# Attention scores: the low-query product on half the array, two query blocks at a time

## The chip, the cores and the metric

The kernel runs on one core of one Trainium2 chip. The metric is device time in microseconds of one execution. A core has TensorE (PE, the matrix multiplier, with its weight loads listed apart as PEld), VectorE (DVE), ScalarE (ACT), GpSimd (POOL) and SyncE (SP, whose queue issues the DMAs). Matmuls read SBUF and write banks of PSUM.

## The reference

One decoder layer for 2048 tokens of width 1024: a norm, one input projection, a causal convolution group beside an attention group, an output projection and a gated feed-forward part. Only the attention's scores are touched. Attention has 8 heads of 64 channels and no softmax:

```python
z = jnp.einsum("bhqd,bhkd->bhqk", qb, kh) * scale
mask = key_pos[None, :] < q_pos[:, None]
log_beta = jax.nn.log_sigmoid(z)
log_1m_beta = jnp.where(mask, jax.nn.log_sigmoid(-z), 0.0)
between = lax.cumsum(log_1m_beta, axis=3, reverse=True) - log_1m_beta
attn = jnp.where(mask, jnp.exp(log_beta + between), 0.0)
return jnp.einsum("bhqk,bhkd->bhqd", attn.astype(vh.dtype), vh)
```

So each query's weights over its keys follow from a running product of 1 - sigmoid(z), from the nearest key backwards.

## The kernel before

Precision: matmuls run on float32 in a rounded form (F32R). A value is split into a high part, rounded, and a low part, what is left; most products are the sum of three matmuls, high-high, high-low and low-high.

Tiling: tokens go in four groups of 512 (`G`, `NG`), each of four blocks of 128 (`TT`). The main stream of PE's work is written by `PLAN`: input projections of a group (`inproj`, lines 624 to 628), output projections (lines 1060 to 1062), first products of the feed-forward part (`c11`, `p4`, line 1124). Beside it run side streams at a set pace: attention (`attn`), the convolution's taps on VectorE (line 845), and sums of weights on GpSimd.

Attention of group g goes by units: one head h and one key group c, from c = g down to 0. There are 80 units, each of four query blocks. `begin(h)` loads the queries Q of a head (line 909), `fetch(h, c)` loads keys K and values V (lines 916 and 917). `scores(u, j)` makes one query block's 128 x 512 scores z in a bank of PSUM (two buffers) with two matmuls, lines 927 and 928, takes a sigmoid of it on ScalarE (line 930) and scans it on VectorE (line 933 on the diagonal, line 935 off it) into a row `om`, of which there are `NOM` buffers. On the diagonal (c = g), block j has (j + 1) x 128 columns. The scan starts with the last column of the same block's scan in the unit before. `values(u, b)` transposes a unit's four rows, 128 columns of each at a time (line 953), splits the result (lines 616 and 617) and multiplies it with V into o (lines 958 and 959). Values lag one unit behind scores.

In DRAM the keys of two heads lie in `kd[p, g]`, 128 channels by (high, low) by 512 tokens; `inproj` writes them with one DMA for the high half and one for the low (line 826). K is read so that its 128 partitions hold channel 0 high, channel 0 low, channel 1 high and so on. Q has each query channel on two neighbouring partitions, for the high half and, beside it, the low half of the queries. So one matmul over 128 partitions gives low queries times (high + low keys), the other high queries times (high + low keys).

The order in which instructions stand on every engine is worked out at build time, once, by a list scheduler (`Graph`, `forward`, `backward`, `arrange`). It works with a cost for each instruction (`cost`), with delays between engines, with a model of the DMAs, and with the buffers of each tile (`grant`): an instruction whose tile finds no free buffer is set aside. `in_order` then fixes that order. `o.after` are the instructions that must have ended before o, `o.behind` those of its own engine that must have been issued before it.

After scores and values end, some 1030 us of the span remain: the last output projection and the feed-forward part, which the diff doesn't touch.

Of the kernel before, what the change touches and what calls it, by code (L numbers as in the profile page):

```python
# [10 lines left out]
F32 = mybir.dt.float32  # L11
F32R = mybir.dt.float32r
# [7 lines left out]
P = 128  # L20
# [12 lines left out]
CW = 31  # L33
PAD = CW - 1
EPS = 1e-6
NOM = 8

PLAN = (
    ("prep", 0, 6, ("scaled", 0, 0, 0)),
# [100 lines left out]
HOP = 60.0  # L140
FLIGHT = 8
ROUNDS = 12
OVER = (("attn", "late"), ("mixed", "ffnt"), ("psum", "fpsum"))


# [51 lines left out]
def cost(i, kind, eng, ins, outs):  # L197

    n = width(outs[0])
    if kind == "InstMatmult":  # L200
        if size_of(ins[0].dtype) == 4 and not str(ins[0].dtype).endswith("r"):
            return 109, 270
        b = max(width(ins[0]) * 0.443, 109)
        return b, b + 165
    src = [place(a) for a in ins]
    if eng == "Activation":
        b = n * 0.833 + (49 if src[0] == "PSUM" else 94) + (93 if len(ins) > 1 else 0)
        return b, b + 115
    if eng == "DVE":
        if kind == "InstTensorScalarPtr":  # L210
            if i.is_tensor_tensor_scan:
                b = 2.04 * n + 140
            elif i.is_scalar_tensor_tensor:
                b = 1.04 * n + 125
            else:
                b = 1.04 * n + 160 if place(outs[0]) == "PSUM" else 0.73 * n + 113
        elif kind == "InstBNStatsAggregate":
            b = 93
        elif kind in ("InstTensorReduce", "InstBNStats"):
            b = 1.04 * width(ins[0]) + 48  # L220
        elif kind == "InstTensorTensor":
            b = 1.04 * n + 60
        else:
            b = n + 100
        return b, b + 100
    if kind == "InstTensorTensor" and n >= 16:
        b = 2.35 * n + 35
    elif "pow" in str(getattr(i, "op", "")):
        b = 375 + 150 * n
    else:  # L230
        b = 125 if n < 16 else 215
    return b, b + 65
# [7 lines left out]
class Op:  # L240
    def __init__(self, n, ins, eng, dma, busy, late, size, wide):
        self.n, self.ins, self.eng, self.dma, self.wide = n, ins, eng, dma, wide
        self.busy, self.late, self.size = busy, late, size
        self.after, self.behind, self.tiles = set(), set(), set()


class Graph:


    def __init__(self, insts):  # L250
        self.ops, self.root, self.order, self.users = [], {}, {}, {}
        seen = {}
        for i in insts:
            kind = type(i).__name__
            ins = [a for a in i.ins if hasattr(a, "bass_ap")]
            outs = [a for a in i.outs if hasattr(a, "bass_ap")]
            if not outs:
                continue
            eng, dma = str(i.engine).split(".")[-1], kind == "InstDMACopy"
            busy, late = (ISSUE, 0) if dma else cost(i, kind, eng, ins, outs)  # L260
            o = Op(len(self.ops), i, eng, dma, busy, late, width(outs[0]) * int(outs[0].ap[0][1]) * 4,
                   eng in ("DVE", "Pool") and not dma and in_sbuf(eng, ins, outs))
            uses = [(a.bass_ap.tensor, box(a), place(a), w) for aps, w in ((ins, False), (outs, True)) for a in aps
                    if hasattr(a.bass_ap.tensor, "tag_meta")]
            for t, b, sp, w in uses:
                if sp != "DRAM" and t.name not in o.tiles:
                    o.tiles.add(t.name)
                    self.users.setdefault(t.name, []).append(o.n)
                    if t.name not in self.root:
                        self.root[t.name] = t  # L270
                        self.order.setdefault(t.tag, []).append(t.name)
                writes, reads = seen.setdefault(t.name, ([], []))
                for old, lst in ((True, writes), (False, reads if w else ())):
                    for q, c, wrote in lst:
                        if sp == "PSUM" or meet(b, c):
                            same = q.eng == eng and not q.dma
                            (o.behind if same and (eng == "PE" or not (old and wrote)) else o.after).add(q.n)
            for t, b, sp, w in uses:
                writes, reads = seen[t.name]
                if sp == "PSUM":  # L280
                    writes[:] = [e for e in writes if e[0].eng != eng] + [(o, b, w)]
                elif w:
                    writes[:] = [e for e in writes if not holds(b, e[1])] + [(o, b, True)]
                    reads[:] = [e for e in reads if not holds(b, e[1])]
                else:
                    reads.append((o, b, False))
            o.behind -= o.after
            self.ops.append(o)
        for low, high in OVER:
            under = {o.n for o in self.ops if any(self.pool(x) == low for x in o.tiles)}  # L290
            for x in self.root:
                if self.pool(x) == high:
                    for n in self.roots(x):
                        self.ops[n].after |= {q for q in under if q < n} - self.ops[n].behind
        self.slots()
# [24 lines left out]

    def forward(self, ops, prio, slots=True):

        need = [len(o.after) + len(o.behind) for o in ops]
        fin = [{} for _ in ops]
        iss = [[] for _ in ops]
# [171 lines left out]
def layer_kernel(ctx: ExitStack, tc: tile.TileContext, x, xT, g_pre_mix, w_in, conv_w, conv_b, ln_g, ln_b,  # L497
# [183 lines left out]
    for g in range(NG):  # L681
        for p in range(CB):
            qd[p, g] = dp.tile([P, 2, G], F32R, name=f"qd{p}_{g}")
            kd[p, g] = dp.tile([P, 2, G], F32R, name=f"kd{p}_{g}")
            vd[p, g] = dp.tile([P, 2, G], F32R, name=f"vd{p}_{g}")

    done = set()
# [90 lines left out]
    def inproj(g, order):  # L778
# [6 lines left out]
        for n, (kind, c) in enumerate(order):  # L785
# [34 lines left out]
            else:  # L820
                H = ev("qkH", F32R)
                L = ev("qkL", F32R)
                split(ps, H, L)
                to = (qd if kind == "q" else kd)[c, g]
                for a, t in enumerate((H, L)):
                    nc.sync.dma_start(to[:, a, :].bitcast(F32), t.bitcast(F32))
            if kind != "v":
                done.add((kind, g, c))
            yield 1
# [70 lines left out]
    def attn(g):  # L900
# [4 lines left out]
        def begin(h):  # L905
            Q = ap.tile([P, 2, G], F32R, tag="Q", name="Q")
            half = qd[h // 2, g][h % 2 * DH:(h % 2 + 1) * DH]
            for i in range(2):
                nc.sync.dma_start(Q[slice(i, P, 2), :, :].bitcast(F32), half.bitcast(F32))
            return dict(Q=Q, prev=[lower[:, 0:1]] * TT, o=None)  # L910

        def fetch(h, c):
            K = ap.tile([P, G], F32R, tag="K", name="K")
            V = ap.tile([P, G], F32R, tag="V", name="V")
            half = kd[h // 2, c][h % 2 * DH:(h % 2 + 1) * DH].rearrange("p a t -> (p a) t")
            nc.sync.dma_start(K.bitcast(F32), half.bitcast(F32))
            nc.sync.dma_start(V.bitcast(F32), vd[h // 2, c][:, h % 2, :].bitcast(F32))
            return dict(h=h, c=c, K=K, V=V, A=[])

        def scores(u, j):  # L920
            hd_ = heads[u["h"]]
            diag = u["c"] == g
            w = (j + 1) * P if diag else G
            K = u["K"]
            z = pp.tile([P, G], F32, tag="z", name="z")
            js = slice(j * P, (j + 1) * P)
            nc.tensor.matmul(z[:, 0:w], hd_["Q"][:, 1, js], K[:, 0:w], start=True, stop=False)  # L927
            nc.tensor.matmul(z[:, 0:w], hd_["Q"][:, 0, js], K[:, 0:w], start=False, stop=True)  # L928
            om = ap.tile([P, G], F32, tag="om", name="om", bufs=NOM)
            nc.scalar.activation(z[:, 0:w], z[:, 0:w], AF.Sigmoid, scale=-0.125)  # L930
            r, zr = (t[:, 0:w][:, ::-1] for t in (om, z))
            if diag:
                nc.vector.tensor_tensor_scan(r, lower[:, G - w:G][:, ::-1], zr, hd_["prev"][j], ALU.add, ALU.mult)
            else:
                nc.vector.tensor_tensor_scan(r, zr, one.to_broadcast([P, w]), hd_["prev"][j], ALU.mult,  # L935
                                             ALU.bypass)
            hd_["prev"][j] = om[:, 0:1]
            if w == P and g:
                hd_["prev"][j] = sp.tile([P, 1], F32, tag="pv", name="pv", bufs=2)
                nc.gpsimd.tensor_tensor(hd_["prev"][j], om[:, 0:1], lower[:, G - P - 1:G - P], ALU.add)  # L940
            u["A"].append(om)
            return w
# [56 lines left out]
        for n in range(len(units) + 1):  # L999
# [6 lines left out]
                u = fetch(h, c)  # L1006
            for i in range(TT):
                w = 0
                if u is not None:
                    w += scores(u, i)  # L1010
                if last is not None:
                    w += values(last, i)
# [795 lines left out]
```

## Time and profile before

| what | value |
| --- | --- |
| time, median of 3 runs | 2353.0 us (2352.53 to 2353.67) |
| the profiled execution | 2352.9 us, span 2351.1 us |
| granted TensorE clock | 0.999 |
| score matmuls, lines 927 and 928 | 320 each, from 66 to 1315 us |
| K and V loads | 80 each, 256 KB |
| data moved by DMA | 656.66 MB |

The page lists an engine's busy time as a share of the span. Matmuls overlap in the array and their ends are modelled, so a matmul's own duration is longer than the time after which the next one can follow. The chain that ended last follows the work back from the last instruction, at each step to what released it; in order of time it shows how long each link of the chain took. A table by stretch gives each engine's busy time between two moments, the granted clock, the share of time in which the DMA engines were busy, and GB/s.

### The profile page before, as it was taken

The page shows a single profiled execution, that of the slowest core. Times are in us where ns is not written, and L with a number is a line of the kernel's source. Part 1 is how long each engine was busy: PE and PEld are TensorE (multiplying, and loading weights), DVE is VectorE, ACT ScalarE, POOL GpSimd, SP SyncE. Part 2 cuts the span into 40 slices and gives each one's busy share as a digit, 9 for nine tenths or more (in the row PEclk, how much of TensorE's full clock was granted, in tenths as well). Part 3 has the DMA queues.
Part 4 walks back from the last instruction along what each step waited for, and adds up shares of the span by engine and source line. Part 5 has one row for each costly group of instructions (what it writes and reads, how often), then busy time and mean ns, then how long its engine had stood idle before and what let it go on. Part 6 is the DMA issues. An engine that isn't in the chain of part 4 may idle for free.

```text
span 2351.1 us, 33675 instructions
## 1 busy us (share of the span) xinstructions
PE 2328.0 (99%) x11156; PEld 1926.8 (82%) x11156; DVE 1720.7 (73%) x2125; ACT 1176.6 (50%) x2102; POOL 1228.2 (52%) x1046
## 2 busy tenths in 40 slices
PE   8999999999999999999999999999999999999998
PEld 6888888888888878888888888888888888888886
DVE  7996899799997899856631268788666564557556
ACT  5457565575564555566564544334232335454543
POOL 4574357523552434335300257679876445478556
PEclk9999999999999999999999999999999999999999
DMA  9989886988698899977598868899998667668765
GB/s 372 310 312 314 300 286 209 348 303 289 226 342 299 285 348 333 331 238 237 180 348 259 271 230 304 301 317 334 366 338 279 207 241 228 195 197 299 228 190 179
DMA packets 277646, 656.66 MB, mean 279 GB/s; under 512 B 32864, under 2 KB 33376, under 8 KB 277472
## 3 DMA queue, kind: packets, MB, share of 16 engines
q1 hardware_dynamic: 277472, 654.51, 81.6%
q8 instruction: 88, 1.44, 0.2%
q14 instruction: 86, 0.70, 0.1%
HBM read 460.40 MB, written 193.99 MB: 278 GB/s over the span
## 4 chain that ended last, share of the span: by engine, by line
PE 96%; DVE 2%; POOL 1%; issue 1%; DMA 0%; ACT 0%; SPq 0%; POOLq 0%; DVEq 0%
PE b L1124 21%; PE dps L1124 17%; PE c L1124 10%; PE inps L624 6%; PE inps L628 6%; PE inps L626 6%; PE at L953 5%; PE z L928 3%; PE o L958 3%; PE o L959 3%; PE z L927 3%; PE p L1124 3%; PE ops L1060 3%; PE ops L1062 3%; PE ops L1061 2%; PE pf L974 1%
## 5 line engine op out<-in xcount | busy, mean ns | idle before, releaser
L845 DVE SCALAR_TENSOR_TENSOR cv<-glu,cw,cv 128x512 f32<-128x512 f32 x464 | 347.7, 749 | 9.5
L1414 POOL TENSOR_TENSOR wL<-raw,wH 128x512 fp32r<-128x512 f32 x176 | 266.3, 1537 | 148.8 <-ACT wH L1413 137.6
L1644 DVE TENSOR_TENSOR xL__19905<-t__19907,xH__19904 128x512 fp32r<-128x512 f32 x154 | 199.7, 1298 | 159.0 <-ACT xH__19904 L1643 158.7
L1642 POOL TENSOR_TENSOR xL__19903<-t__19906,xH__19902 128x512 fp32r<-128x512 f32 x154 | 208.5, 1356 | 157.5 <-ACT xH__19902 L1641 156.1
L617 DVE TENSOR_TENSOR TL<-at,TH 128x512 fp32r<-128x512 f32 (+1 forms) x320 | 189.3, 599 | 122.2 <-ACT TH L616 109.0
L578 ACT ACTIVATE wH<-raw 128x1024 fp32r<-128x1024 f32 x156 | 165.4, 1060 | 214.7 <-PE inps L628 105.5
L624 PE MATMUL inps<-xH,wL 128*128 128x512 f32 x640 | 257.8, 403 | 1.0 <-DVE glu L797 0.4
L626 PE MATMUL inps<-xH,wH 128*128 128x512 f32 x640 | 254.6, 398 | 0.0
L628 PE MATMUL inps<-xL,wH 128*128 128x512 f32 x640 | 254.3, 398 | 0.0
L935 DVE TENSOR_TENSOR_SCAN om<-z,om,one 128x512 f32<-128x512 f32 x168 | 212.8, 1274 | 42.9 <-ACT z L930 38.7
L1124 PE MATMUL dps<-xH__19902,xL__19905 128*128 128x512 f32 x616 | 239.8, 389 | 0.2 <-DVE xL__19905 L1644 0.2
L1124 PE MATMUL dps<-xH__19902,xH__19904 128*128 128x512 f32 x616 | 239.5, 389 | 0.0
L1124 PE MATMUL dps<-xL__19903,xH__19904 128*128 128x512 f32 x616 | 239.1, 389 | 0.0
L616 ACT ACTIVATE TH<-at 128x512 fp32r<-128x512 f32 (+1 forms) x320 | 167.9, 532 | 90.7 <-PE at L953 81.8
L930 ACT ACTIVATE z<-z 128x512 f32<-128x512 f32 (+2 forms) x320 | 167.4, 528 | 70.8 <-PE z L928 66.6
L1641 ACT ACTIVATE xH__19902<-t__19906 128x512 fp32r<-128x512 f32 x154 | 97.2, 631 | 205.5 <-POOL xL__19903 L1642 162.5
L582 POOL TENSOR_TENSOR wL<-raw,wH 128x1024 fp32r<-128x1024 f32 x46 | 110.5, 2402 | 149.0 <-ACT wH L578 122.2
L1413 ACT ACTIVATE wH<-raw 128x512 fp32r<-128x512 f32 x176 | 101.7, 624 | 163.7 <-PE b L1124 55.8
L953 PE MATMUL at<-idr,om 128*128 128x128 f32 x1088 | 180.8, 273 | 0.5 <-DVE om L935 0.4
L953 PEld LDWEIGHTS at<-idr,om 128*128 128x128 f32 x1088 | 136.4, 140 | 34.7 <-DVE om L935 0.9
L1208 POOL TENSOR_TENSOR sum<-sum 128x512 f32<-128x512 f32 x88 | 115.1, 1308 | 60.0 <-DMA sum<-in_w_gate_dram 40.7
L1124 PE MATMUL c<-xH,wL 128*128 128x512 f32 x352 | 140.8, 401 | 0.1
(296 smaller groups left out, 6014.0 us busy)
## 6 DMA issues: line engine op xcount, KB each, us to landing
wL<-wL SPq DMA_DIRECT2D x156, 512.0 KB, 5.2
raw<-in_w_in_dram SPq DMA_DIRECT2D x80, 512.0 KB, 6.1
t__19907<-u SPq DMA_DIRECT2D x154, 256.0 KB, 3.1
c<-c SPq DMA_DIRECT2D x88, 256.0 KB, 4.7
t__19906<-wd SPq DMA_DIRECT2D x88, 256.0 KB, 2.7
K<-kd SPq DMA_DIRECT2D x80, 256.0 KB, 4.6
V<-vd SPq DMA_DIRECT2D x80, 256.0 KB, 4.3
u<-accf SPq DMA_DIRECT2D x22, 768.0 KB, 6.7
```

Source lines behind the costliest of these rows:

```text
L616: nc.scalar.activation(H, ps, AF.Copy)
L617: nc.vector.tensor_tensor(L, ps, H.bitcast(F32), ALU.subtract)
L624: nc.tensor.matmul(ps, WL[:, kc], aH[t](k), start=k == 0, stop=False)
L626: nc.tensor.matmul(ps, WH[:, kc], aH[t](k), start=False, stop=False)
L628: nc.tensor.matmul(ps, WH[:, kc], aL[t](k), start=False, stop=k == KT - 1)
L845: nc.vector.scalar_tensor_tensor(to, gl[c][:, k:k + G], cw[:, c, k:k + 1], a, ALU.mult, ALU.add)
L935: nc.vector.tensor_tensor_scan(r, zr, one.to_broadcast([P, w]), hd_["prev"][j], ALU.mult, ALU.bypass)
L953: nc.tensor.transpose(pt[:, j * P:(j + 1) * P], u["A"][j][:, b * P:(b + 1) * P], id32)
L1124: return nc.tensor.matmul(ps, a, b, skip_group_check=True, **flags)
L1414: nc.gpsimd.tensor_tensor(l, t, f32(h), sub)
L1642: nc.gpsimd.tensor_tensor(WL, w, f32(WH), sub)
L1644: nc.vector.tensor_tensor(UL, t, f32(UH), sub)
```

## The change

The two matmuls of a block become a full and a half one. K's 128 partitions now hold the 64 high key channels and below them the 64 low ones; Q has the query channels twice, on partitions 0 to 63 and 64 to 127. High queries meet all 128 partitions, as before in sum. Low queries meet high keys alone, 64 partitions; the product of low queries and low keys is left out. `scores` is called for two blocks at a time: first the high matmul of either block, then the low matmul of block j on partitions 0 to 63, and that of block j + 1 on partitions 64 to 127, for which a second copy of the high keys (`KX`, two buffers) is loaded there. The two low matmuls write different banks. `NOM` goes from 8 to 6. Keys lie in DRAM by head (`kd[h, g]`), so that each tile of them is written by four DMAs. The scheduler takes a matmul whose operand starts above partition 0 as beside the matmul ahead of it, keeps it directly behind that one, and reckons 15 ns for it (`BESIDE`).

```diff
-NOM = 8
+NOM = 6
+BESIDE = 15.0
...
     if kind == "InstMatmult":
...
+        if box(ins[1])[0]:
+            return BESIDE, BESIDE + 165
...
+            if kind == "InstMatmult" and box(ins[1])[0]:
+                o.beside = True
+                last.after |= o.after
+                last.behind |= o.behind - {last.n} - last.after
+                last.behind -= last.after
+                o.after, o.behind = set(), {last.n}
+            if eng == "PE":
+                last = o
...
+        if slots:
+            prio = [float("-inf") if o.beside else prio[o.n] for o in ops]
...
-            kd[p, g] = dp.tile([P, 2, G], F32R, name=f"kd{p}_{g}")
+            for h in (2 * p, 2 * p + 1):
+                kd[h, g] = dp.tile([P, G], F32R, name=f"kd{h}_{g}")
...
-                to = (qd if kind == "q" else kd)[c, g]
                 for a, t in enumerate((H, L)):
-                    nc.sync.dma_start(to[:, a, :].bitcast(F32), t.bitcast(F32))
+                    if kind == "q":
+                        nc.sync.dma_start(qd[c, g][:, a, :].bitcast(F32), t.bitcast(F32))
+                        continue
+                    for h in range(2):
+                        nc.sync.dma_start(kd[2 * c + h, g][a * DH:(a + 1) * DH, :].bitcast(F32),
+                                          t[h * DH:(h + 1) * DH, :].bitcast(F32))
...
-                nc.sync.dma_start(Q[slice(i, P, 2), :, :].bitcast(F32), half.bitcast(F32))
+                nc.sync.dma_start(Q[slice(i * DH, (i + 1) * DH), :, :].bitcast(F32), half.bitcast(F32))
...
-            half = kd[h // 2, c][h % 2 * DH:(h % 2 + 1) * DH].rearrange("p a t -> (p a) t")
-            nc.sync.dma_start(K.bitcast(F32), half.bitcast(F32))
+            nc.sync.dma_start(K.bitcast(F32), kd[h, c].bitcast(F32))
+            KX = ap.tile([P, G], F32R, tag="KX", name="KX", bufs=2)
+            nc.sync.dma_start(KX[DH:P, :].bitcast(F32), kd[h, c][0:DH, :].bitcast(F32))
...
-            w = (j + 1) * P if diag else G
-            K = u["K"]
-            z = pp.tile([P, G], F32, tag="z", name="z")
-            js = slice(j * P, (j + 1) * P)
-            nc.tensor.matmul(z[:, 0:w], hd_["Q"][:, 1, js], K[:, 0:w], start=True, stop=False)
-            nc.tensor.matmul(z[:, 0:w], hd_["Q"][:, 0, js], K[:, 0:w], start=False, stop=True)
+            Q, K, KX = hd_["Q"], u["K"], u["KX"]
+            zs = []
+            for i in (j, j + 1):
+                w = (i + 1) * P if diag else G
+                z = pp.tile([P, G], F32, tag="z", name="z")
+                zs.append((i, w, z, slice(i * P, (i + 1) * P)))
+            for i, w, z, js in zs:
+                matmul(z[:, 0:w], Q[:, 0, js], K[:, 0:w], start=True, stop=False)
+            for (i, w, z, js), hp, k in zip(zs, (slice(0, DH), slice(DH, P)), (K, KX)):
+                matmul(z[:, 0:w], Q[hp, 1, js], k[hp, 0:w], start=False, stop=True)
+            return sum([scan(u, hd_, diag, *z) for z in zs])
+
+        def scan(u, hd_, diag, j, w, z, js):
             om = ap.tile([P, G], F32, tag="om", name="om", bufs=NOM)
...
-                if u is not None:
+                if u is not None and i % 2 == 0:
                     w += scores(u, i)
```

More of the change, by code (lines that the diff above doesn't have):

```diff
@@ L243, in __init__ @@
         self.busy, self.late, self.size = busy, late, size
-        self.after, self.behind, self.tiles = set(), set(), set()
+        self.after, self.behind, self.tiles, self.beside = set(), set(), set(), False
 class Graph:
@@ L914, in fetch @@
             V = ap.tile([P, G], F32R, tag="V", name="V")
-            half = kd[h // 2, c][h % 2 * DH:(h % 2 + 1) * DH].rearrange("p a t -> (p a) t")
-            nc.sync.dma_start(K.bitcast(F32), half.bitcast(F32))
+            nc.sync.dma_start(K.bitcast(F32), kd[h, c].bitcast(F32))
+            KX = ap.tile([P, G], F32R, tag="KX", name="KX", bufs=2)
+            nc.sync.dma_start(KX[DH:P, :].bitcast(F32), kd[h, c][0:DH, :].bitcast(F32))
             nc.sync.dma_start(V.bitcast(F32), vd[h // 2, c][:, h % 2, :].bitcast(F32))
-            return dict(h=h, c=c, K=K, V=V, A=[])
+            return dict(h=h, c=c, K=K, KX=KX, V=V, A=[])
         def scores(u, j):
```

## The prediction

> **What bounds the kernel now.** I read the page first: busy time by engine, then the chain that ended last.
>
> ```profile
> PE 2328.0 (99%) x11156; PEld 1926.8 (82%) x11156; DVE 1720.7 (73%) x2125; ACT 1176.6 (50%) x2102; POOL 1228.2 (52%) x1046
> PE 96%; DVE 2%; POOL 1%; issue 1%; DMA 0%; ACT 0%; SPq 0%; POOLq 0%; DVEq 0%
> PE z L927 <- DVE om L935: 0.8, 2, 0.5
> ```
>
> The matmuls make up 96% of the chain. The third row, from the list of who waited for whom, says that scores waited for a free bank of PSUM twice, 0.8 us in all. A busy PE is a modelled figure, so the next view is the table by stretch, which shows whether the other engines leave room where scores run (66 to 1315 us).
>
> ```profile
> core 0: us, PE busy (x) PEld busy (x) DVE busy (x) ACT busy (x) POOL busy (x), PEclk, DMA share, GB/s
> 66.00:1315.00 1249.00, 1245.94 (x6364) 1033.93 (x6363) 999.99 (x1356) 707.13 (x1274) 515.00 (x505) 1.00 0.85 289
> 200.00:1000.00 800.00, 798.03 (x4109) 661.27 (x4108) 730.44 (x991) 454.04 (x818) 355.64 (x346) 1.00 0.87 299
> 800.00:1000.00 200.00, 198.26 (x1000) 162.62 (x1000) 188.02 (x249) 102.06 (x181) 81.26 (x50) 1.00 0.95 330
> 1000.00:1315.00 315.00, 315.00 (x1561) 261.26 (x1560) 148.91 (x181) 178.73 (x312) 78.02 (x82) 1.00 0.75 252
> ```
>
> PE is idle for 3.1 of 1249 us. VectorE is 91% busy from 200 to 1000 (730.44 of 800), 94% in the last 200 of these, and has room only after 1000. So a microsecond taken from PE's stream in this stage is a microsecond of the end, as long as VectorE and the DMAs follow.
>
> How much stream time one matmul takes is read from the chain in order of time (start, length, what), not from an instruction's own duration, which holds the latency too:
>
> ```profile
> 702.37 0.12 PE z L927
> 702.49 0.12 PE z L928
> 703.24 0.18 PE z L928
> 1315.46 3.18 PE c L1124 x14
> 1318.64 0.44 PE at L953 x4
> 1319.08 2.09 PE c L1124 x9
> 1312.24 2.32 PE c L1124 x10
> 1325.94 3.00 PE c L1124 x13
> ```
>
> 512 columns take 3.18 / 14 = 0.227 us; z of 384 columns takes 0.18 (703.24), of 256 takes 0.12 (702.37), and a transpose of 128 columns 0.44 / 4 = 0.11. The granted clock is 1.00 in all these stretches, so no term changes with it.
>
> **The matmuls that go beside each other.** The groups by form count them:
>
> ```profile
> L927 PE MATMUL z<-K,Q 128*128 128x512 f32 x224 | 94.0, 419 | 0.9 <-DVE om L935 0.8
> L927 PE MATMUL z<-K,Q 128*128 128x384 f32 x32 | 11.9, 373 | 0.0
> L927 PE MATMUL z<-K,Q 128*128 128x256 f32 x32 | 10.3, 323 | 0.0
> L927 PE MATMUL z<-K,Q 128*128 128x128 f32 x32 | 7.7, 240 | 0.0
> ```
>
> There are 320 score blocks, each with a low and a high matmul (L928 has the same counts). The number of matmuls stays. The high ones keep 128 partitions and the stacked high and low keys; each low one drops to 64 partitions and loses the low-low product. Two neighbouring blocks make a pair, and the second low one sits on the other partition half, with no data in common with the first. If they run at once, a pair costs the longer of the two. Per head and key group off the diagonal there are two pairs of 512 and 512 columns: 224 less the 32 diagonal ones is 192 blocks, 96 pairs, saving 0.227 each: 21.8 us. On the diagonal, 32 pairs of 384 and 512 save the 384 one, 0.18 each: 5.8 us. 32 pairs of 128 and 256 save the 128 one, taken at a transpose's 0.11: 3.5 us. Together 31.1 us over 160 pairs: the most that there is.
>
> No instruction of before uses half the array (all forms read 128*128), so whether halves overlap, and at what price, is bounded. There are two unknowns.
>
> First, the second half's own weight load. Loads in the trace, near a stretch of transposes:
>
> ```profile
> 1318.25 0.58 PEld L953 LDWEIGHTS at<-idr,om 128*128 128x128 f32 x4
> 1318.81 0.19 PEld L1124 LDWEIGHTS c<-xH,wL 128*128 128x128 f32 x1
> 1318.92 0.19 PEld L1124 LDWEIGHTS c<-xH,wH 128*128 128x128 f32 x1
> 1319.15 0.19 PEld L1124 LDWEIGHTS c<-xL,wH 128*128 128x128 f32 x1
> ```
>
> Two loads can start 0.11 us apart (1318.81, 1318.92), though behind a long matmul each follows at the matmul's 0.23. So the second low matmul starts between 0 and 0.11 late. I take 0: the last high matmul streams for 0.227 in most pairs, and two loads of 0.11 fit under it. The other end is 160 x 0.11 = 17.6 us.
>
> Second, going from the whole array to halves and back. The nearest row is PE's other change of work, four transposes between plain matmuls: after them nine matmuls take 2.09 us where 9 x 0.227 = 2.04 is due, ten take 2.32 for 2.27, thirteen 3.00 for 2.95. A visit costs 0.05. The far end is that the pipe empties at each change: a matmul lasts 0.39 from start to end while its successor comes 0.23 later, so 0.16 a change and 0.32 a pair:
>
> ```profile
> 1304.30 0.39 PE L927 MATMUL z<-K,Q 128*128 128x512 f32 x1
> 1304.52 0.39 PE L928 MATMUL z<-K,Q 128*128 128x512 f32 x1
> ```
>
> The near end is nothing, as halves need not stop anything. I take 0.05, the one price of a change that the trace holds: 160 x 0.05 = 8.0 us.
>
> The rule that speaks against the change stands in the Trainium skill, TensorEngine Tiling (Array Packing), Key Properties: changing the tiling mode drains the engine. No run shown here changes it; at 0.16 a drain the sum would be 31.1 - 51.2, a loss of 20 us, which is the first rival. The page TensorE: Matmul & The Clock Gate, "Measured speedup vs the span model", has tiles on different rows starting about 4 ns apart: an estimate of 160 x 0.004 = 0.6 us for the second halves, against my 0.
>
> **The other parts.** *The order on PE.* The first high, the second high, then both low; the planner sets the second low matmul directly behind the first. Both banks of z are now held together: the next pair's first high matmul needs the first scan done, the low ones need both. Between the end of a pair's second scan and the next pair's first scan lie high, low and latency (0.23 + 0.39) and a sigmoid, some 1.2 us. What bears this is time per unit of four blocks: 80 units between 66 and 1315 us, 15.6 us each.
>
> ```profile
> L935 DVE TENSOR_TENSOR_SCAN om<-z,om,one 128x512 f32<-128x512 f32 x168 | 212.8, 1274 | 42.9 <-ACT z L930 38.7 <-PE at L953 3.3
> L617 DVE TENSOR_TENSOR TL<-at,TH 128x512 fp32r<-128x512 f32 x224 | 151.1, 680 | 103.6 <-ACT TH L616 91.9 <-PE o L959 8.5 <-PE at L953 1.4
> L930 ACT ACTIVATE z<-z 128x512 f32<-128x512 f32 x224 | 131.5, 592 | 45.1 <-PE z L928 41.3 <-issue 1.8 <-ACT qkH L616 0.7
> ```
>
> A full unit's work on VectorE is 4 x 1.27 + 4 x 0.68 = 7.8 us, and twice 1.2 added still leaves 5 us for the rest. Cost: 0.
>
> *Six weight rows for eight.* A unit's blocks 2 and 3 can't be scanned before the previous unit's values have read its four rows. Up to now a whole unit could run ahead, now half. Covered by the same 15.6 us; without that cover PE waits for z as in the row of 0.8 us. Cost: 0, with the danger costed as a rival.
>
> *DMA.* Each unit fetches 128 KB more (the second copy, 80 of them, 10.5 MB), and each of the 16 key tiles is written as four quarters of 128 KB in place of two transfers of 256 KB: 32 more issues. SP's queue issues one in about 0.32 us, so 112 more take 36 us of its time, spread over 1249; the copy stands between K and V in it, so V starts 0.3 us later. The transfers:
>
> ```profile
> K<-kd SPq DMA_DIRECT2D x80, 256.0 KB, 4.6
> V<-vd SPq DMA_DIRECT2D x80, 256.0 KB, 4.3
> Q<-qd SPq DMA_DIRECT2D x64, 256.0 KB, 5.5
> 824.85 2.62 DMA V<-vd
> ```
>
> 10.5 MB beside 289 GB/s x 1249 us = 361 MB is 3%, in a stage that the DMAs fill to 0.85, and units are fetched a unit ahead, 15.6 us for some 5. Cost: 0. If the cover is gone it shows as that last row does, a unit's fetch on the chain: 0.3 us of later issue for the dozen units between 800 and 1000 would be 4 us. Q's rows go to two blocks of 64 partitions where they went to every second partition: same bytes, same number of transfers, landing at 5.5 before; 0.
>
> *VectorE and ScalarE* have the same instructions. If 23 us leave PE, some 70% of it from 200 to 1000, VectorE there is at 730 / 784 = 93%, and what it can't finish moves behind 1000, where it has 166 us free.
>
> **The sum.** 31.1 - 8.0 - 0 = 23.1 us. The profiled execution took 2352.9 us, with a span of 2351.1 and 1.8 around it, 0.1 from the median of 2353.0. 2352.9 - 23.1 = 2329.8, so 2330.
>
> **The rivals.**
> 1. *The array empties at each change (slower).* Place: before the first low matmul and before the next full one. Price 0.16 each by the latency above. It decides at 31.1 / 160 = 0.19 us a pair, 0.10 a change; at 0.16 the time is 2352.9 + 20.1 = 2373. For it: 0.39 against 0.23 shows that there is something to drain. Against: PE's change to transposes costs 0.05, not 0.3.
> 2. *The halves don't overlap.* Then the change takes nothing away: 2352.9 and, with 0.05 a visit, up to 2361. Nothing in the trace excludes it.
> 3. *The second half waits for its own weights*, 0.11 each: 31.1 - 8.0 - 17.6 = 5.5, giving 2347. For it: behind long matmuls loads run one ahead only. Against: nothing but the rows of 0.11.
> 4. *PE is freed and something else ends last*: scans held by six rows and paired banks, or VectorE at 94%. If what is saved before 1000 us (70%) is lost, 7 us remain: 2346. For it: 91% and 94%; against: the room after 1000 and PE's waits of under 1 us.
>
> **How the numbers follow.** My forecast has 0.52: overlap with a change priced from 0 to 0.1 a pair, so 2321.8 to 2338, its own range. Rival 1 has 0.15, rival 2 0.10, rival 3 0.11, rival 4 0.12. What can be told from no change is 0.2%, 4.7 us. Faster: 0.52, rival 4's 0.11 and 0.08 of rival 3, 0.71. Same: what is left of these, 0.04, and half of rival 2, 0.05: 0.09. Slower: 0.15 and the other 0.05, 0.20. The range goes from 2320 (nothing paid, and a little for another order) to 2361, the end of rival 2; the far part of rival 1 is left out.
>
> **What would show it.** Right: the two low matmuls start under 0.05 us apart, on forms of 64 partitions; the chain's step from a pair's first low matmul to the next full one is 0.23 to 0.28; scores' share of the chain, 3% and 3% now, falls to about 4.5%; PE's idle time from 66 us to scores' end stays near 3 us; what comes after scores has the same length. Rival 1: the step is over 0.42. Rival 2: starts 0.23 apart. Rival 3: starts 0.11 apart. Rival 4: PE waits for om, TL or a DMA for several microseconds. Two prices make the prediction wrong: the change of array, and a new order of the plan, which shifts work on all queues.

## The result, and the profile after

The change made the kernel slower: 2393.6 us against 2353.2, ratio 1.0172, 95% interval 1.0159 to 1.0185. The profiled execution has a span of 2392.7 us, 41.6 more than before.

From the page after: busy time by engine, and the chain by engine.

```profile
PE 2363.0 (99%) x11156; PEld 1895.7 (79%) x11156; DVE 1717.8 (72%) x2125; ACT 1177.8 (49%) x2102; POOL 1229.1 (51%) x1046
PE 93%; DVE 2%; issue 1%; DMA 1%; POOL 1%; ACT 1%; SPq 0%; POOLq 0%; DVEq 0%; ACTq 0%
```

PE has the same number of instructions and is as full as before, yet busy for 35 us more. VectorE, ScalarE and GpSimd do what they did. So it is PE's own stream that became longer. Where, the table by stretch shows. First the kernel before, in three parts: from 59 us to the end of the last value, the 67 us behind it, and the rest:

```profile
59.00:1334.00 1275.00, 1271.94 (x6488) 1055.46 (x6487) 1010.80 (x1372) 721.04 (x1297) 523.09 (x512) 1.00 0.85 289
1334.00:1401.00 67.00, 66.91 (x298) 54.64 (x297) 36.48 (x40) 37.21 (x62) 32.43 (x26) 1.00 0.70 241
1401.00:2351.00 950.00, 940.02 (x4159) 777.12 (x4157) 631.13 (x659) 383.53 (x693) 644.24 (x465) 1.00 0.78 263
```

The changed kernel in the same three parts:

```profile
59.00:1375.00 1316.00, 1306.85 (x6489) 1024.15 (x6488) 1009.37 (x1371) 723.42 (x1299) 524.68 (x512) 1.00 0.87 289
1375.00:1442.00 67.00, 66.89 (x298) 54.65 (x297) 36.33 (x40) 37.26 (x63) 32.37 (x25) 1.00 0.70 241
1442.00:2392.00 950.00, 940.14 (x4160) 777.25 (x4158) 630.12 (x659) 383.31 (x693) 644.84 (x466) 1.00 0.78 263
```

Up to the last value the same 6488 matmuls, but for one, take 41 us more, which is the whole loss, with PE idle for 9.2 us where it was 3.1. Behind it nothing differs: 298 matmuls in 67 us in both, then 940 us of PE in 950 in both.

The groups by form show what PE does now (L1150 is the line of a helper through which the scores' matmuls go in this kernel):

```profile
L1150 PE MATMUL z<-K,Q 128*128 128x512 f32 x224 | 86.2, 412 | 3.1 <-DVE om L961 3.1
L1150 PE MATMUL z<-KX,Q 64*128 64x512 f32 x128 | 63.6, 497 | 0.0
L1150 PE MATMUL z<-K,Q 64*128 64x512 f32 x96 | 47.7, 496 | 0.0
```

The half matmuls are there as intended, 64 partitions by 128 columns, but each lasts 0.50 us where a full one of the same 512 columns lasted 0.39. Now one visit, in the timeline of PE and its weight loads (start, length, what):

```profile
704.22 0.19 PEld L1150 LDWEIGHTS z<-K,Q 128*128 128x128 f32 x1
704.44 0.82 PE L1150 MATMUL z<-K,Q 128*128 128x512 f32 x2
704.76 0.18 PEld L1150 LDWEIGHTS z<-K,Q 64*128 64x128 f32 x1 [0.35 <-issue]
704.76 0.18 PEld L1150 LDWEIGHTS z<-KX,Q 64*128 64x128 f32 x1
704.76 0.50 PE L1150 MATMUL z<-KX,Q 64*128 64x512 f32 x1
705.19 0.19 PEld L639 LDWEIGHTS inps<-xH,wH 128*128 128x128 f32 x1 [0.25 <-issue]
705.19 0.50 PE L639 MATMUL inps<-xH,wH 128*128 128x512 f32 x1
705.53 0.39 PE L641 MATMUL inps<-xL,wH 128*128 128x512 f32 x1
```

The row of 704.44 holds two matmuls, the second high one and the first low one, which ends at 705.26, together with the second low one (704.76 + 0.50). So the halves do overlap, completely. But the loads of both halves start only at 704.76, after 0.35 us in which the load side did nothing. A plain successor would have begun at 704.44 + 0.23 = 704.67. And the full matmul behind the pair again loads its weights in the open, from 705.19, and lasts 0.50. The chain adds it up:

```profile
704.61 0.66 PE z L1150 x3
705.26 0.43 PE inps L639
705.69 0.23 PE inps L641
```

0.66 for the second high matmul and the pair is 0.43 more than a stream time of 0.23, and the next full matmul takes 0.43 for 0.23: a visit costs 0.20 going in and 0.20 coming out.

### The profile page after: what moved, and what is told of

The parts are those of the page before. It is cut to its first block, busy times and chain, and to the rows that moved or that the text cites. A ratio compares the mean times of both kernels' runs of the same rounds, so it can differ in the third digit from the quotient of the medians.

```text
span 2392.7 us, 34018 instructions
## 1 busy us (share of the span) xinstructions
PE 2363.0 (99%) x11156; PEld 1895.7 (79%) x11156; DVE 1717.8 (72%) x2125; ACT 1177.8 (49%) x2102; POOL 1229.1 (51%) x1046
## 4 chain that ended last, share of the span: by engine, by line
PE 93%; DVE 2%; issue 1%; DMA 1%; POOL 1%; ACT 1%; SPq 0%; POOLq 0%; DVEq 0%; ACTq 0%
PE b L1150 21%; PE dps L1150 17%; PE c L1150 10%; PE inps L637 6%; PE inps L639 6%; PE inps L641 6%; PE z L1150 5%; PE at L979 5%; PE p L1150 3%; PE ops L1086 3%; PE o L985 3%; PE ops L1088 3%; PE ops L1087 2%; PE o L984 2%; PE pf L1000 1%
## 5 line engine op out<-in xcount | busy, mean ns | idle before, releaser
L1150 PE MATMUL dps<-xH__20110,xL__20113 128*128 128x512 f32 x616 | 239.8, 389 | 0.2 <-DVE xL__20113 L1670 0.2
L1150 PE MATMUL dps<-xH__20110,xH__20112 128*128 128x512 f32 x616 | 239.5, 389 | 0.0
L1150 PE MATMUL dps<-xL__20111,xH__20112 128*128 128x512 f32 x616 | 239.1, 389 | 0.0
L956 ACT ACTIVATE z<-z 128x512 f32<-128x512 f32 (+2 forms) x320 | 154.8, 518 | 107.2 <-PE z L1150 96.1
L979 PE MATMUL at<-idr,om 128*128 128x128 f32 x1088 | 189.1, 275 | 1.0 <-DVE om L961 0.4
L595 POOL TENSOR_TENSOR wL<-raw,wH 128x1024 fp32r<-128x1024 f32 x46 | 111.3, 2419 | 149.4 <-ACT wH L591 120.0
L1150 PE MATMUL z<-K,Q 128*128 128x512 f32 (+3 forms) x480 | 172.5, 402 | 3.1 <-DVE om L961 3.1
```

Source lines behind the costliest of these rows:

```text
L979: nc.tensor.transpose(pt[:, j * P:(j + 1) * P], u["A"][j][:, b * P:(b + 1) * P], id32)
L1150: return nc.tensor.matmul(ps, a, b, skip_group_check=True, **flags)
```

## The experiments

Theory A: the loss is the price of the visits, 160 x 0.40 - 31.1 = 32.9 us, and little else. Theory B: it is the order, that is paired banks, six weight rows and the added transfers. Theory C: a half matmul is slow by itself.

**No visits: low matmuls on the whole array.**

```diff
-            for (i, w, z, js), hp, k in zip(zs, (slice(0, DH), slice(DH, P)), (K, KX)):
-                matmul(z[:, 0:w], Q[hp, 1, js], k[hp, 0:w], start=False, stop=True)
+            for i, w, z, js in zs:
+                matmul(z[:, 0:w], Q[:, 1, js], K[:, 0:w], start=False, stop=True)
```

> The low matmuls run on all 128 partitions again (low queries with high and low keys); pairing, six weight rows, the second copy of the high keys and its transfers stay. Theory A (all of the loss comes with the changes between whole and half array, 0.20 us in and 0.20 us out of each of 160 visits): no visits are left, nothing overlaps, so the time before, 2353, within 5 us. Theory B (the loss comes from two banks held together, six rows or the added transfers): it keeps most of the 40 us, 2380 to 2394.

2359.1 us, ratio 1.0023 (1.0014 to 1.0032). Nearly all of the loss is gone with the half matmuls alone; pairing, six rows and the copy stayed. It is 1 us above the range of A and 21 below that of B: 35 of 40 us go with the half matmuls, 5 us are left for B. The order is new as well, so the 35 hold whatever the order of the changed kernel lost beside its visits.

**Two visits a pair**, each low matmul behind its own high one:

```diff
             for (i, w, z, js), hp, k in zip(zs, (slice(0, DH), slice(DH, P)), (K, KX)):
+                matmul(z[:, 0:w], Q[:, 0, js], K[:, 0:w], start=True, stop=False)
                 matmul(z[:, 0:w], Q[hp, 1, js], k[hp, 0:w], start=False, stop=True)
```

(The loop of the high matmuls and the scheduler's rule for a second half are taken out.)

> Each low matmul stands behind its own high matmul, on its own half, so the array is changed for each of 320 blocks and nothing overlaps. Theory A: 2353 + 320 x 0.40 = 2481, within 15 us. Theory B: only the lost overlap is added to the changed kernel, 2394 + 31 = 2425 or less. Theory C (a half-array matmul is slow by itself, 0.43 us instead of 0.23, with no price for the change): 2353 + 320 x 0.2 = 2417.

2468.1 us, ratio 1.0486 (1.0465 to 1.0507): 13 us under A's 2481, far above the others. In its chain a whole pair, high, low, high, low, where the planner left it together:

```profile
701.52 1.52 PE z L1147 x4
703.04 0.59 PE at L976 x4
```

1.52 is 0.23 + 3 x 0.43: every change costs its 0.20, in either direction. Four transposes behind it take 0.59 where 0.44 is usual, 0.15 more, so coming out into transposes is a little cheaper. Summed over the whole trace, from the end of each matmul to the end of the next and less its stream time, the ways in and out of the 320 visits come to 121 us and not 128, 0.38 a visit. That is 7 of the 13 us; the rest wasn't followed.

**Each visit's pair twice** (the low product is added twice; the scheduler keeps the four matmuls together):

```diff
+            for n in range(2):
                 for (i, w, z, js), hp, k in zip(zs, (slice(0, DH), slice(DH, P)), (K, KX)):
-                matmul(z[:, 0:w], Q[hp, 1, js], k[hp, 0:w], start=False, stop=True)
+                    matmul(z[:, 0:w], Q[hp, 1, js], k[hp, 0:w], start=False, stop=n == 1)
```

> The two low matmuls of a pair are issued twice in one visit (the low product is added twice, which the reference does not do): one more overlapping pair in half-array mode, no further change of mode. Theory A: the second pair costs only its stream time, 128 x 0.227 + 32 x 0.12 = 33 us, so 2394 + 33 = 2427, and in the chain a visit's matmuls take 0.23 us more. Theory C: each overlapping pair costs 0.43, 160 x 0.43 = 69 us more, 2463. If the halves did not overlap, 66 us more, 2460.

2416.6 us, ratio 1.0267 (1.0247 to 1.0288), 23 above the changed kernel. The timeline of a visit:

```profile
702.96 0.18 PEld L1152 LDWEIGHTS z<-KX,Q 64*128 64x128 f32 x1
702.96 0.49 PE L1152 MATMUL z<-KX,Q 64*128 64x512 f32 x1
703.06 0.19 PEld L1152 LDWEIGHTS z<-K,Q 64*128 64x128 f32 x1
703.07 0.19 PEld L1152 LDWEIGHTS z<-KX,Q 64*128 64x128 f32 x1
703.29 0.39 PE L1152 MATMUL z<-K,Q 64*128 64x512 f32 x1
703.29 0.39 PE L1152 MATMUL z<-KX,Q 64*128 64x512 f32 x1
```

And the chain's row for it:

```profile
702.80 0.89 PE z L1152 x5
```

Within the visit the second pair's loads go ahead under the first pair (703.06, 703.07), both its matmuls start at once and last 0.39, and the visit takes 0.89 for 0.66: two matmuls more in one stream time. C is out: only the change is dear. By the visits' arithmetic alone the time would be 2353.2 + 64.0 - 31.1 + 32.9 = 2419; it is 2 below that. I expected 2427 because I started from 2394, which holds what the changed kernel loses beside its visits. This one loses less there: PE is idle for 4.7 us up to the last value (1339.00 less 1334.26), not 9.2.

**Both low matmuls on the same half:**

```diff
-                matmul(z[:, 0:w], Q[hp, 1, js], k[hp, 0:w], start=False, stop=True)
+                matmul(z[:, 0:w], Q[0:DH, 1, js], K[0:DH, 0:w], start=False, stop=True)
```

(The scheduler keeps the two together and reckons the second at its full time.)

> Both low matmuls of a pair use partitions 0 to 63 (the same half of queries and of keys), one behind the other in one visit. If two halves overlap because they lie on different rows, as theory A has it, nothing overlaps here and a visit lasts one stream time more: 31 us above the changed kernel's 2394, 2425, within 6 us; the two low matmuls end 0.23 us apart. If any two half matmuls overlapped, or none did before, 2394.

2417.0 us, ratio 1.0269 (1.0251 to 1.0288), 8 under what I expected and outside its range, again because I started from 2394. By the arithmetic of the visits alone it is 2353.2 + 64.0 = 2417. That it fits to the microsecond is luck, as PE has idle time of its own here (6.6 us: 1339.00 less 1332.41). The chain:

```profile
705.53 0.88 PE z L1151 x3
706.41 0.43 PE inps L642
```

0.88 for 0.66: without different rows there is no overlap. So the gain of 0.22 a pair was real, and was outspent.

**Narrower weights**, 72 of 128 query columns (the low product of the other 56 queries is left out):

```diff
-                matmul(z[:, 0:w], Q[hp, 1, js], k[hp, 0:w], start=False, stop=True)
+                matmul(z[0:72, 0:w], Q[hp, 1, js][:, 0:72], k[hp, 0:w], start=False, stop=True)
```

> The low matmuls use 72 of a block's 128 queries (the low product of the other 56 is left out), so that their weight load has 72 columns and not 128; stream time and visits stay. Theory A1 (a change into halves costs 0.20 because the array first runs empty, 0.09, and the weights are then loaded in the open, 0.11): the load shrinks to 0.06, the low matmul's duration in the trace from 0.50 to 0.45, and 160 x 0.05 = 8 us come back, 2386. Theory A2 (0.20 is waiting for the array alone, the load is hidden): duration 0.50 and 2394.

2387.8 us in two runs of 2385.7 and 2390.0; ratio 1.0145 (1.0127 to 1.0164). The time leans to A1, and the timeline decides:

```profile
707.01 0.14 PEld L1150 LDWEIGHTS z<-K,Q 64*72 64x72 f32 x1 [0.35 <-issue]
707.02 0.45 PE L1150 MATMUL z<-KX,Q 64*72 64x512 f32 x1
```

The chain of the same visit:

```profile
706.86 0.61 PE z L1150 x2
707.46 0.43 PE inps L641
```

0.45 for 0.50, 0.61 for 0.66 on the way in, and 0.43 on the way out, where the full matmul's weights still have 128 columns. So the price of 0.20 has two parts: the weight load in the open (0.11 for 128 columns, 0.06 for 72) and 0.09 before it, from the end of the last matmul's stream to the start of the load (704.67 to 704.76 above).

**96 partitions**, neighbours on the same rows:

```diff
-                matmul(z[:, 0:w], Q[hp, 1, js], k[hp, 0:w], start=False, stop=True)
+                matmul(z[:, 0:w], Q[0:96, 1, js], K[0:96, 0:w], start=False, stop=True)
```

> The low matmuls use 96 of the 128 partitions (low queries with the high keys and half of the low keys), one behind the other, no overlap. If the price hangs on a change of the array's division and 96 rows need the whole array, there is no price: as with the whole array, 2359 within 5 us, durations of 0.39. If any other number of rows than before has the price, 160 visits at 0.40: 2417 to 2425.

2360.8 us, ratio 1.0031 (1.0019 to 1.0042). Its groups by form:

```profile
L1150 PE MATMUL z<-K,Q 96*128 96x512 f32 x224 | 85.9, 401 | 0.0
```

0.40 us: no price. So it isn't the smaller number of rows as such that costs: 96 are free, 64 are not. Numbers between them weren't run.

**Pairs off the diagonal alone**, 96 visits:

```diff
+                if diag:
+                    hp, k = slice(0, P), K
```

> Half matmuls in pairs off the diagonal alone: 96 visits in place of 160, each of which saves 0.227 and costs 0.40; diagonal blocks on the whole array. Theory A: 96 x 0.17 = 17 us above 2353 to 2359, so 2370 to 2376. If the loss came from a few bad places in the order and not from each visit, it could be anywhere from 2359 to 2394, with PE waits of several microseconds where it is high.

2370.1 us, ratio 1.0071 (1.0048 to 1.0093): 96 x 0.173 = 16.6 above 2353.5 is 2370.1. Along the number of visits: 0, 2359; 96, 2370; 160, 2394. The steps are 11 and 23 us where the arithmetic of the visits has 16.6 and 16.3, so the number of visits alone doesn't give the times. PE's idle time differs too:

```profile
59.00:1351.00 1292.00, 1287.92 (x6488) 1030.44 (x6487) 1003.71 (x1371) 726.43 (x1298) 524.01 (x512) 1.00 0.88 294
```

That is 4.1 us with 96 visits, against 9.2 with 160.

**The scheduler told the price**, 0.20 us more for either half (the costs alone are changed):

```diff
-            return BESIDE, BESIDE + 165
+            return BESIDE + 200, BESIDE + 165
         b = max(width(ins[0]) * 0.443, 109)
+        if box(ins[1])[1] == DH:
+            b += 200
```

> Same instructions as the changed kernel; the list scheduler is told 0.20 us more for the first low matmul of a pair and 0.20 more for the second, what the trace shows, so only the order can change. Theory A with the visits worth 160 x 0.40 - 31 = 33 us: the other 8 us of the loss come from an order planned for a faster PE, and 3 to 8 us come back, 2386 to 2391. Theory B (six rows and paired banks bound the order): no change, 2391 to 2397.

2395.7 us, ratio 1.0179 (1.0162 to 1.0196): no gain. That lies in the range of B, but not for B's reason. The new order has another hole of its own, in the list of waits:

```profile
PE po L1019 <- DVE ot L1011: 7.7, 1, 7.7
```

Where it lies, the granted clock (the third number from the end) falls as well:

```profile
156.00:160.00 4.00, 0.00 (x0) 0.00 (x0) 4.00 (x1) 0.66 (x2) 4.00 (x6) 0.68 1.05 263
160.00:164.00 4.00, 1.10 (x5) 1.04 (x5) 4.00 (x3) 0.00 (x0) 2.30 (x2) 0.50 0.58 230
164.00:168.00 4.00, 4.00 (x17) 3.48 (x15) 3.93 (x8) 3.60 (x7) 2.53 (x2) 0.54 0.02 4
```

So the true cost doesn't win the remainder back. Whether the wrong one had brought it about isn't decided, as one hole took the place of another.

**The rest of the change without half matmuls and without the copy**, with eight rows and with six:

```diff
-NOM = 6
+NOM = 8
...
-            KX = ap.tile([P, G], F32R, tag="KX", name="KX", bufs=2)
-            nc.sync.dma_start(KX[DH:P, :].bitcast(F32), kd[h, c][0:DH, :].bitcast(F32))
```

> Both low matmuls on the whole array as in the kernel without half matmuls (2359), eight weight rows as before, and no second copy of the high keys: what is left of the change is that two blocks go together and that both banks of z are held, with the new layout of Q and K. If the 5 us that the kernel without half matmuls lost against before come from six rows or from the copy's transfers, this is at 2354. If they come from pairing alone, 2359.

> The same with six weight rows, still without the second copy. If the copy's 10.5 MB cost the 5 us: 2354. If six rows cost them: 2359 while eight rows give 2354. If it is pairing: 2359 in both.

Eight rows: 2352.8, ratio 0.9996 (0.9987 to 1.0005). Six rows: 2356.2, ratio 1.0012 (1.0003 to 1.0020). So pairing, both banks of z held together and the new layout (a tile of keys for each head, written by two DMAs) cost nothing. Six rows go with some 3 us, the copy with another 3 (2359.1 - 2356.2). Each is a new order as well, so neither is more than the difference of two orders.

## Why the prediction was wrong

The step that failed is the second unknown, "going from the whole array to halves and back", which I took at 0.05 us a pair and which measures 0.40. I chose the row nearest to it as transposes between plain matmuls. But those run on 128*128 like the rest, so PE changes its work there and not its division. The rows of before held no price for the division at all, and the honest bound was the far one: pair by pair 0.32, not 0.05.

The far end and rival 1 were too low as well. Rival 1 had the mechanism, the place and the point where it decides (0.10 a change), with 0.16 for a change and 2373. It counted a pipe running empty but not that the next weights then can't be loaded ahead. That is the sentence in the first unknown, "two loads of 0.11 fit under it": the loads of both halves start at one moment (704.76), so the second half is not late at all, 0 as taken, but neither is under the last high matmul. The step from the first low matmul to the next full one is 705.19 - 704.76 = 0.43 us, which is the sign that the prediction gave for rival 1 (over 0.42). With 0.20 a change the sum is 31.1 - 64.0 = -32.9 and 2352.9 + 32.9 = 2385.8.

Of the 40.4 us, 32 to 33 are thus the visits: 32.9 by the chain's steps at one visit, and 32 when the steps of all matmuls in the trace, each less its stream time, are added (ways in 30, ways out 30, less 28 for the overlaps). The other 7 to 8 belong to the terms that I put at nothing. The 5 us that I counted as left in a unit's 15.6 were not free: VectorE was busy for 730.44 of 800 us, that is 14.2 of each 15.6, so its other work fills them. One place in the changed kernel shows PE waiting for it: VectorE's queue (scan, taps, splits) holds the chain from 572.6 to 578.8 us. The first and last of its rows there, and two of the matmuls that follow:

```profile
572.61 0.29 DVE TL L630
...
578.22 0.60 DVE TL L630
...
580.94 0.43 PE inps L637
...
584.82 0.23 PE inps L639
```

The table by stretch (the third number from the end is the granted clock):

```profile
574.00:578.00 4.00, 1.94 (x5) 0.75 (x5) 4.00 (x6) 0.97 (x3) 1.27 (x1) 0.93 0.85 240
578.00:582.00 4.00, 3.13 (x9) 2.58 (x10) 4.00 (x8) 1.57 (x4) 0.00 (x0) 0.50 0.83 196
582.00:586.00 4.00, 4.00 (x15) 3.15 (x14) 2.57 (x5) 0.00 (x0) 0.00 (x0) 0.72 0.89 283
```

Five matmuls run in 4 us, then the granted clock is 0.50 and a matmul takes 0.43 us (580.94) until it is back (584.82). By the three rows the clock was at 0.50 for 0.6 + 4 + 2.2 = 6.8 us. That is rival 4 in small, and a term that the prediction left out when it took the clock for 1.00 throughout.

The size of the remainder fits what the rows show. PE's idle time up to the last value grew by 6.1 us, and 6.8 us at half the clock lose at most 3.4, partly the same time: at most 9.5 us for the 7 to 8. With 96 visits, six rows and the copy PE idles only 1 us more than before, and nothing is left of the remainder (2370.1 against 2370.1). By size, then, the remainder is PE's waiting and the lower clock in the order of the changed kernel. In the kernel without half matmuls six rows and the copy account for about 5. How much of the waiting is six rows, the copy or the luck of an order stays open.

What was right: PE bounds the stage and its microseconds count in full; the size of the overlap (0.22 a pair of 512 columns in the chain, where the sum had 0.227); the two halves starting together; no cost from the paired banks or the new layout; nothing changed after the last value.

I set aside the rule of the Trainium skill, TensorEngine Tiling (Array Packing), Key Properties, that changing the tiling mode drains the engine. The trace agrees in the main: 0.09 us of waiting in each direction, and 0.11 of load behind it, which the rule doesn't name. That the array is empty by then isn't shown: by its modelled end (704.44 + 0.39 = 704.83) the last full matmul is still 0.07 us from done when the halves load.

The Trainium skill, TensorE: Matmul & The Clock Gate, "LDWEIGHTS (loading the stationary operand)", has the load's time go by columns and not by rows. The trace agrees: 0.11 at 128 columns, on 64 rows going in as on 128 coming out, and 0.06 at 72 columns on 64 rows.

## What to carry to other kernels

Count how often a stream of full matmuls would change to half the array, not only how much the halves overlap: here a visit cost 0.40 us and a pair in it saved 0.23, while a second pair in the same visit took only 0.23 for two matmuls. By these figures a visit with 512 columns pays from two pairs on, just (0.45 saved for 0.40), which wasn't run; here two score banks allow one pair. When the trace has no row for an operation, a neighbour that merely looks like a change is no estimate: keep the far end as the likeliest until a row shows the thing itself.

## What the runs showed of the hardware

- From the whole array to halves and back: 0.20 us each way at a visit of 512 columns, of it 0.09 before the weight load starts and 0.11 for a load of 128 columns; 0.38 for both ways in the mean of 320 visits. 96 rows have no price (0.40 us for 512 columns, 0.39 to 0.42 with 128).
- Two halves on different rows load their weights at the same moment (704.76) and end together; on the same half they follow each other at 0.22.
- Where PE had little to do the granted clock fell to 0.50: in the changed kernel for 6.8 us (five matmuls from 574 to 578 us), with matmuls at 0.43 in place of 0.23; with the scheduler told the price for some 10 us (no matmul from 156 to 160).
